# A hybrid attention and RG-LRU layer: each engine's order from a list scheduler in the kernel, in place of orders set by hand

## The chip, the cores and the metric

The kernel runs on one core of one Trainium2 chip. A core has five engines that run their own instruction streams in order and wait for each other through semaphores: PE (TensorE, matmuls; PEld is its weight loading), DVE (VectorE), ACT (ScalarE), POOL (GpSimd) and SP (SyncE, which only issues DMAs here). The metric is the device time in microseconds (us).

## The reference

One decoder layer on 2048 tokens of width 1024, in float32 (BATCH = DEPTH = 1). A mixer of eight attention heads and an RG-LRU recurrence share one input and one output projection; an MLP follows; both have RMS norms before and after.

```python
def hybrid_mixer(h, ...):
    z = h @ w_in                                   # 1024 x 2560
    q, k, v, xr, gr = jnp.split(z, [512, 1024, 1536, 2048], axis=-1)
    attn = dilated_attention(q, k, v)              # 8 heads of 64, patterns (128,1), (512,4), (2048,16)
    xr = causal_depthwise_conv(xr, conv_w, conv_b) # width 4
    rec = rg_lru(xr, w_r, b_r, w_i, b_i, lam) * jax.nn.gelu(gr)
    return jnp.concatenate([attn, rec], axis=-1) @ w_out

def rg_lru(x, ...):   # gates from block-diagonal products of x
    r = sigmoid(x @ w_r + b_r); i = sigmoid(x @ w_i + b_i)
    log_a = -8.0 * r * softplus(-lam)
    a = exp(log_a); u = sqrt(-expm1(2 * log_a)) * (i * x)
    # h[t] = a[t] * h[t-1] + u[t], an associative scan over the sequence

def reference(x, ...):
    h = rms_norm(x, mix_norm_pre)
    x = x + rms_norm(hybrid_mixer(h, ...), mix_norm_post)
    h = rms_norm(x, mlp_norm_pre)
    a = jax.nn.relu(h @ w1)                        # 1024 x 4096
    return x + rms_norm((a * a) @ w2, mlp_norm_post)
```

## The kernel before

**Products.** A float32 product is made of three matmuls: each operand is split into a high and a low part (fp32r), and high*high, high*low and low*high are added up in PSUM. The split is a cast on ACT for the high part (`split`, L54) and a subtraction on DVE or POOL for the low part (L55). wH, wL are a weight's parts, hH, hL those of the scaled input, thA, tlA, thB, tlB those of the attention probabilities.

**Tokens.** They are handled in two halves (hf 0 and 1) of 1024, each in two blocks b of 512. z_ct_b is a product of the input projection: column tiles 0 to 3 of 128 give q, 4 to 7 k, 8 to 11 v, 12 to 15 xr, 16 to 19 gr. Each has 8 x 3 matmuls of 512 columns (L198 to L200). The norm in front of it is applied afterwards: x is loaded in rows (xn, L145) for the sums of squares, `spread_norm` turns them into a broadcast tile bc with four small matmuls (pbc, L187), and bc multiplies the finished product. The operands themselves come from x transposed (xr_k, L167, eight loads of 256 KB for each block) and the gain g_sb.

**Recurrence** (`recurrent`). For each channel group c and block b: product 12+c, xr (DVE, L304), a first tap of the convolution on POOL (L307), three multiply-adds on DVE (xc, L310), the gate matmuls pr and pi on xc (L313, L315; their operands are plain float32), tanh, exp and sqrt on ACT, a scan on DVE (L331), and the gated output ge (L335 to L343, partly on POOL).

**Attention.** Per head, part A (S, local windows) and part B (SB, dilated): scores on PE (L557, L614, L615), row maximum with mask on DVE (L414), exponential on ACT (L420), transposes on PE (pT, L393), split on ACT and DVE, products with the values on PE (oA L581, oB L640), fold on ACT and DVE (L409). Halves of scores are numbered S_head_n and SB_head_c.

**The rest.** Output projection (m, L857 to L859), norm, then the MLP, whose first product (za, zb, zc, L1072 to L1074) and second product (o, L1222 to L1224) are each made by seven products of half-size blocks. The second half's attention runs while the first half's o products are under way.

**What sets the order.** The code writes steps in the order of three strings, with the letters q (a group of q, k and v products), r (a recurrence group), x (load and norm of a block) and a (a pair of heads):

```python
ORDER = "q00 r02 q01 a0 r03 q02 a1 q03 x2 x3 a2 q10 a3"
BETWEEN = "r10 r11 r12 r13"
LATER = "q11 q12 q13"
```

A scheduler of the framework that simulates a timeline (`schedule_with_timeline_sim=True`) orders the instructions of each engine from there. Two constructs override it. `tc.manual_schedule(engines=...)` keeps the code's own order: for PE from the output projection of the first half on, and for ACT, DVE and SP too while `interleave` mixes the second half's attention units with the first half's o products by counts written by hand. `tc.issue_after(ins)` keeps the instructions issued in it behind `ins` on the same engine. After that each engine works through its list in order.

## Time and profile before

| | |
|---|---|
| Runs | 2236.11 us median of 3 (2228.41, 2236.11, 2237.35) |
| Profiled execution | 2235.21 us; span from first to last instruction 2233.4 us |
| Mean granted TensorE clock | 0.988 |
| HBM traffic | read 337.09 MB, written 151.13 MB |
| Matmuls waited most for | gate products pr (L313), first operands of z (L198), values oB (L640) |

The time is that of the whole execution, the span ends with the last instruction; the two differ by 1.8 us. "Busy" counts the time in which an engine has an instruction under way; PE's matmuls overlap in the pipeline, so a matmul of 512 columns is listed with about 400 ns while the next starts some 225 ns after it.

### The profile page before, as it was taken

What the parts mean: (1) busy time and instruction counts of PE and PEld (TensorE: products, weight loads), DVE (VectorE), ACT (ScalarE), POOL (GpSimd) and SP (SyncE); (2) the same over time, 40 slices, a digit from 0 to 9 for tenths busy, and PEclk for the clock granted to TensorE, in tenths of its full rate; (3) what the DMA queues carried; (4) which work ended last, traced back from release to release, by engine and by line L of the source; (5) the groups of instructions that cost most, each with busy time, mean ns of one, the idle gap of its engine ahead of it and who ended that gap; (6) DMA issues with size and microseconds to landing.
All of it is one profiled execution on the core that took longest, in us unless ns stands there. A gap on an engine that the chain in (4) does not pass through costs nothing.

```text
span 2233.4 us, 30770 instructions
## 1 busy us (share of the span) xinstructions
PE 2155.4 (97%) x10264; PEld 1775.5 (79%) x10264; DVE 1507.1 (67%) x2910; ACT 1230.3 (55%) x2489; POOL 453.3 (20%) x536
## 2 busy tenths in 40 slices
PE   8999989989999999999999999999999999999998
PEld 6678878768788788888788787778878888888887
DVE  6767565987748867775667677778766566646456
ACT  7646464655434555554666666754455555654442
POOL 5543414555323000000001111113200000000003
PEclk9999999999999999999999999999999999999999
DMA  8365684555974676878777777777553434776665
GB/s 289 100 189 177 182 243 145 171 169 161 330 254 160 216 292 251 303 269 307 216 222 223 209 235 225 230 232 229 184 187 127 175 134 165 288 227 195 192 196 179
DMA packets 224116, 473.51 MB, mean 212 GB/s; under 512 B 23428, under 2 KB 78756, under 8 KB 217684
## 3 DMA queue, kind: packets, MB, share of 16 engines
q1 hardware_dynamic: 195140, 337.52, 47.9%
q0 software_dynamic: 28816, 134.01, 17.0%
q8 instruction: 81, 1.33, 0.2%
q14 instruction: 79, 0.65, 0.1%
HBM read 337.09 MB, written 151.13 MB: 219 GB/s over the span
## 4 chain that ended last, share of the span: by engine, by line
PE 68%; DVE 12%; DMA 7%; ACT 4%; issue 3%; POOL 1%; SPq 1%; DVEq 0%; ACTq 0%; POOLq 0%
PE o L1223 8%; PE o L1222 8%; PE o L1224 8%; PE za L1073 4%; PE za L1074 4%; PE za L1072 4%; PE z L198 3%; PE z L199 3%; PE z L200 3%; PE m L859 2%; PE m L858 2%; PE m L857 2%; PE zc L1073 2%; PE zc L1072 2%; PE zc L1074 2%
## 5 line engine op out<-in xcount | busy, mean ns | idle before, releaser
L198 PE MATMUL z<-hH,wH 128*128 128x512 f32 x640 | 262.4, 410 | 16.2 <-ACT wH L54 8.6
L199 PE MATMUL z<-hL,wH 128*128 128x512 f32 x640 | 259.7, 406 | 0.0
L200 PE MATMUL z<-hH,wL 128*128 128x512 f32 x640 | 258.7, 405 | 0.5 <-DVE wL L55 0.5
L198 PEld LDWEIGHTS z<-hH,wH 128*128 128x128 f32 x640 | 123.3, 193 | 51.7 <-ACT wH L54 9.2
L199 PEld LDWEIGHTS z<-hL,wH 128*128 128x128 f32 x640 | 123.2, 193 | 29.4 <-issue 4.1
L200 PEld LDWEIGHTS z<-hH,wL 128*128 128x128 f32 x640 | 122.9, 192 | 29.4 <-issue 4.6
L420 ACT ACTIVATE smB<-smB,stB 128x128 f32<-128x128 f32 (+3 forms) x128 | 71.6, 560 | 88.8 <-DVE stB L414 88.7
L1077 ACT ACTIVATE sq<-sq 128x512 f32<-128x512 f32 x93 | 58.8, 633 | 97.5 <-DVE sq L1081 97.5
L55 POOL TENSOR_TENSOR wL<-wraw,wH 128x512 fp32r<-128x512 f32 x58 | 83.3, 1452 | 78.0 <-ACT wH L54 75.2
L55 DVE TENSOR_TENSOR tlB<-pT_B,thB 128x384 fp32r<-128x384 f32 x96 | 57.0, 598 | 51.6 <-ACT thB L54 48.7
L1137 POOL DMA_DIRECT2D sa<-sq x31 | 16.5, 533 | 360.7 <-ACT sq L1078 350.1
L54 ACT CAST wH<-wraw 128x512 fp32r<-128x512 f32 (+1 forms) x81 | 47.2, 611 | 62.7 <-DMA wraw<-in_dram 31.9
L420 ACT ACTIVATE sm<-sm,stA 128x256 f32<-128x256 f32 (+1 forms) x128 | 63.1, 495 | 29.3 <-DVE stA L414 28.9
L1078 ACT ACTIVATE sq<-sq 128x512 f32<-128x512 f32 x124 | 76.1, 628 | 1.8
L1256 POOL TENSOR_TENSOR y<-y,g4b 128x512 f32<-128x512 f32 x8 | 12.4, 1583 | 259.3 <-ACT junk_y L84 259.3
L414 DVE CUSTOM_DVE_ANT_0 smB<-SB,mask_b 128x128 f32<-128x128 f32 (+3 forms) x128 | 59.2, 482 | 7.0 <-PE pT_B L393 6.3
L55 DVE TENSOR_TENSOR tlA<-pT,thA 128x512 fp32r<-128x512 f32 (+1 forms) x64 | 42.3, 669 | 26.1 <-ACT thA L54 25.8
L54 ACT CAST thB<-pT_B 128x384 fp32r<-128x384 f32 x96 | 48.4, 509 | 18.2 <-PE pT_B L393 10.8
L393 PE MATMUL pT_B<-ident,smB 128*128 128x128 f32 x320 | 52.3, 280 | 2.8 <-DVE nb L409 1.7
L414 DVE CUSTOM_DVE_ANT_0 sm<-S,mask_a 128x256 f32<-128x256 f32 (+1 forms) x128 | 47.4, 409 | 9.4 <-PE pT L393 4.0
L1072 PE MATMUL zc<-hHT,f_7H 128*128 128x512 f32 x128 | 50.1, 391 | 2.8 <-ACT hHT L54 2.8
L640 PE MATMUL oB<-thB,vb 128*128 128x256 f32 x192 | 46.5, 273 | 6.2 <-ACT thB L54 5.3
(608 smaller groups left out, 7035.0 us busy)
## 6 DMA issues: line engine op xcount, KB each, us to landing
sa<-as POOLq DMA_DIRECT2D x31, 1024.0 KB, 6.3
w1r<-in_dram SPq DMA_DIRECT2D x56, 512.0 KB, 4.2
sa<-sq POOLq DMA_DIRECT2D x31, 768.0 KB, 4.0
wraw<-in_dram SPq DMA_DIRECT2D x79, 256.0 KB, 3.8
place<-in_dram SPq DMA_DIRECT2D x14, 1024.0 KB, 7.6
sb<-place POOLq DMA_DIRECT2D x14, 1024.0 KB, 5.4
kh<-sk SPq DMA_DIRECT2D x24, 512.0 KB, 5.2
kl<-sk SPq DMA_DIRECT2D x24, 512.0 KB, 6.5
```

Source lines behind the costliest of these rows:

```text
L55: (lo_eng or nc.vector).tensor_tensor(out=lo, in0=src, in1=f32(hi), op=ALU.subtract))
L198: pe.matmul(z, hi[:, k, :], hh, start=(k == 0), stop=False)
L199: pe.matmul(z, hi[:, k, :], hl, start=False, stop=False)
L200: pe.matmul(z, lo[:, k, :], hh, start=False, stop=(k == KT - 1))
L414: v.tensor_tensor_reduce(out=sm[:, c0:c0 + w], in0=sp[:, c0:c0 + w], in1=mask[:, mask.shape[-1] - w:], scale=1.0, scalar=3.0e38, op0=ALU.a ...
L420: s.activation(out=sm[:, c0:c0 + w], in_=sm[:, c0:c0 + w], func=AF.Exp, scale=-1.0, bias=st[:, 0, u, cols[j]:cols[j] + 1], accum_out=st[:, ...
L1072: pe.matmul(o, hi[:, k], bh[:, k], start=start and k == 0, stop=False, skip_group_check=True)
L1073: pe.matmul(o, hi[:, k], bl[:, k], start=False, stop=False, skip_group_check=True)
L1074: pe.matmul(o, lo[:, k], bh[:, k], start=False, stop=k == KH - 1, skip_group_check=True)
L1222: pe.matmul(o, ah[:, ts], bh, start=fresh and j == 0, stop=False, skip_group_check=True)
L1223: pe.matmul(o, ah[:, ts], bl, start=False, stop=False, skip_group_check=True)
L1224: pe.matmul(o, al[:, ts], bh, start=False, stop=j == NJ - 1, skip_group_check=True)
```

## The change

The framework's context is wrapped in a class `Plan`. `manual_schedule` does nothing any more, and `issue_after` only records its pairs. When the whole program has been written, `Plan.run` works out from tiles and addresses which instruction depends on which, and hands them to `Machine`, which simulates the engines with cost formulas of its own (`cost`, `transfer`). At each moment an engine takes, of the instructions that are ready by that simulation, the one with the smallest `need`: the number, in the order of the code, of the first PE instruction that depends on it, directly or through others, or that waits for a buffer that it frees (at most 600 above its own number). A PE instruction's `need` is its own number. Loads whose `need` lies more than 400 PE instructions ahead wait. The resulting order of every engine is then fixed by dependencies from each instruction to the next. What is computed, and with which instructions, stays the same; the added helper lines move line numbers by 2, and those of `trunk` and below by 474.

```diff
+WINDOW = 400
+LAG = 600
+SLACK = 0.8
+BACKLOG = 4.0
...
+class Plan:
...
+    def manual_schedule(self, engines):
+        return contextlib.nullcontext()
+
+    @contextlib.contextmanager
+    def issue_after(self, ins):
+        traced = self.nc.cur_bb.bb.instructions
+        n = len(traced)
+        yield
+        self.behind += [(i.name, ins.name) for i in self.nc.cur_bb.bb.instructions[n:] if i.engine == ins.engine]
...
+    def run(self):
+        ins = [i for i in self.nc.cur_bb.bb.instructions if i.engine in ENGINES and i.outs]
...
+        order = Machine(ins, eng, acc, first, issued, self.taken, self.slots, held, guards).run()
+        info = mybir.DependencyInfo(mybir.DependencyClass.NoSync, mybir.DependencyReason.DATA)
+        for seq in order.values():
+            for a, b in zip(seq, seq[1:]):
+                self.tc.add_manual_dep(ins[b], ins[a].name, info, reason="plan")
...
+class Machine:
...
+        self.need = [n] * n
+        for _ in range(3):
+            for k in reversed(range(n)):
+                after = self.then[k] + [j for g in self.gates[k] for j in self.then[g]] + follow[k]
+                self.need[k] = k if eng[k] == "PE" else min([self.need[j] for j in after], default=n)
+        self.need = [min(x, k + LAG) for k, x in enumerate(self.need)]
...
+    def offer(self, k):
...
+        load = isinstance(self.ins[k], mybir.InstDMACopy) and self.acc[k][-1][6]
+        if load and self.need[k] > self.edge():
+            heapq.heappush(self.far, (self.need[k], k))
+            return
+        heapq.heappush(self.ready[e], (self.need[k], k))
+        self.poke(e)
...
+    def issue(self, e):
...
+        while self.ready[e]:
+            _, k = heapq.heappop(self.ready[e])
...
+        self.order[e].append(k)
...
+    def finish(self, k, pe):
+        slack = SLACK if k < self.n else 0
...
+        for j in self.then[k]:
+            if pe is None and slack and j < self.n and self.eng[j] == "PE":
+                self.at(self.now + slack, self.free_one, j, k)
...
+    def cost(self, k):
...
+            if f:
+                hold = 0.11 if n == P and i.is_transpose else 0.00174 * n
+            else:
+                hold = {P: 0.083, 2 * P: 0.121, 3 * P: 0.174}.get(n, 0.000446 * n)
...
+    def transfer(self, k):
...
+        rate = 6.0 if src[0] and dst[0] else 2.8 if dst[0] else 3.2 if run >= 512 else 4.8
...
     with tile.TileContext(nc, schedule_with_timeline_sim=True) as tc:
-        trunk(tc, *args, out)
+        plan = Plan(tc)
+        trunk(plan, *args, out)
+        plan.run()
```

The orders below are the rows of one engine's instruction list, with line, operation, output and inputs. Numbers behind a name tell tiles apart.

Three places show how instructions move. The first is SP's list at the very start of the program, before. xr_k are the blocks of transposed x, wraw_12 the raw weights of z_12.

```order
L167 DMA xr_0_287<-in_dram 128x512
L169 DMA g_sb<-in_dram 128x8
L126 DMA wraw_12_0_285<-in_dram 128x256
L167 DMA xr_1_297<-in_dram 128x512
L167 DMA xr_2_306<-in_dram 128x512
L167 DMA xr_3_312<-in_dram 128x512
```

The same place now, SP's first eleven rows; xn_j are the rows of x for the sums of squares, of the first block (366 to 375) and of the second (464 to 473).

```order
L147 DMA xn_0_366<-in_dram 128x1024
L147 DMA xn_1_369<-in_dram 128x1024
L147 DMA xn_2_372<-in_dram 128x1024
L147 DMA xn_3_375<-in_dram 128x1024
L169 DMA xr_0_287<-in_dram 128x512
L147 DMA xn_0_464<-in_dram 128x1024
L147 DMA xn_1_467<-in_dram 128x1024
L147 DMA xn_2_470<-in_dram 128x1024
L147 DMA xn_3_473<-in_dram 128x1024
L171 DMA g_sb<-in_dram 128x8
L128 DMA wraw_12_0_285<-in_dram 128x256
```

The eight xn loads have moved ahead of the gain and of the first weights; before, the first of them stood in row 17. PE's list, too, now begins with the four pbc of the first block.

The second place is DVE's list in the first recurrence groups, before, at the convolution of channel group 1, block 1 (xc_1_1). The xr_1_1 that it reads is made in row 89, the rows here are 114 to 121; a, th, i and ge are steps of other groups.

```order
L342 SCALAR_TENSOR_TENSOR ge_0_1_759<-ge_0_1_759,gr_0_1_757 128x512
L330 TENSOR_TENSOR i_0_1_719<-i_0_1_719,th_0_1_721 128x512
L228 TENSOR_TENSOR zn_4_1_1063<-z_4_1_1038,bc_501 128x512
L331 SCALAR_TENSOR_TENSOR xc_0_1_708<-r_0_1_717,state,i_0_1_719 128x512
L310 SCALAR_TENSOR_TENSOR xc_1_1_796<-xr_1_1_792,cw,xc_1_1_796 128x512
L332 COPY state<-xc_0_1_708 128x1
L343 SCALAR_TENSOR_TENSOR ge_0_1_759<-ge_0_1_759,xc_0_1_708 128x512
L310 SCALAR_TENSOR_TENSOR xc_1_1_796<-xr_1_1_792,cw,xc_1_1_796 128x512 x2
```

The same convolution now, rows 102 to 111 of DVE.

```order
L306 TENSOR_TENSOR xr_1_1_792<-z_13_1_767,bc_501 128x4x128
L334 COPY state<-xc_1_0_620 128x1
L345 SCALAR_TENSOR_TENSOR ge_1_0_671<-ge_1_0_671,xc_1_0_620 128x512
L328 TENSOR_TENSOR a_0_1_724<-r_0_1_717 128x512
L331 SCALAR_TENSOR_TENSOR i_0_1_719<-i_0_1_719,xc_0_1_708 128x512
L312 SCALAR_TENSOR_TENSOR xc_1_1_796<-xr_1_1_792,cw,xc_1_1_796 128x512
L329 SCALAR_TENSOR_TENSOR th_0_1_721<-a_0_1_724,th_0_1_721 128x512
L312 SCALAR_TENSOR_TENSOR xc_1_1_796<-xr_1_1_792,cw,xc_1_1_796 128x512
L344 SCALAR_TENSOR_TENSOR ge_0_1_759<-ge_0_1_759,gr_0_1_757 128x512
L312 SCALAR_TENSOR_TENSOR xc_1_1_796<-xr_1_1_792,cw,xc_1_1_796 128x512
```

The three multiply-adds have moved up to within nine rows of their xr_1_1, each with one other step between.

The third place is PE's list in the middle of head 5 of the first half, before; z_16_1 is a product of a recurrence group of the second half.

```order
L615 MATMUL SB_5_2_0_3728<-kl_5_3574,qs_5_3572 128x128
L614 MATMUL SB_5_2_0_3728<-kh_5_3573,qs_5_3572 128x256
L615 MATMUL SB_5_2_0_3728<-kl_5_3574,qs_5_3572 128x256
L199 MATMUL z_16_1_4690<-hL_2_3307,wH_16_4539 128x512
L200 MATMUL z_16_1_4690<-hH_2_3306,wL_16_4540 128x512
L393 MATMUL pT_0_5_1_0_3642<-ident,sm_5_4_3631 128x128 x4
L393 MATMUL pT_0_5_1_1_3659<-ident,sm_5_6_3650 128x128 x4
L198 MATMUL z_16_1_4690<-hH_3_3312,wH_16_4539 128x512
```

The same scores now:

```order
L395 MATMUL pT_0_5_1_0_3642<-ident,sm_5_4_3631 128x128 x2
L617 MATMUL SB_5_2_0_3728<-kl_5_3574,qs_5_3572 128x128
L616 MATMUL SB_5_2_0_3728<-kh_5_3573,qs_5_3572 128x256
L583 MATMUL oA_5_0_3618<-thA_3593,va_2_3359 128x256
L583 MATMUL oA_5_0_3618<-tlA_3594,va_2_3359 128x256
L617 MATMUL SB_5_2_0_3728<-kl_5_3574,qs_5_3572 128x256
```

The products of the recurrence are gone from between the scores, transposes and values of the head: those of heads 4 and 5 stand in rows 1321 to 1517 of PE's list together with 24 matmuls of z_0_0, where before they began in row 1265 and ended in row 1761.

382 lines of the change are left out of this document (added).

## The prediction

> **What bounds the kernel now.** I read the page's busy times and the clock row first, to see how much there is to win at all.
>
> ```profile
> PE 2155.4 (97%) x10264; PEld 1775.5 (79%) x10264; DVE 1507.1 (67%) x2910; ACT 1230.3 (55%) x2489; POOL 453.3 (20%) x536
> core 0: 2233.4 us, clock 0.988
> ```
>
> TensorE (PE) is busy for 2155.4 of 2233.4 us. The change removes no matmul, so two things can shrink: the 78.0 us in which PE idles, and the time its clock was held back, (1 - 0.988) x 2233.4 = 26.8 us of full-speed work. Together they bound any gain at 4.7%.
>
> Next come the windows of 50 us, which show where those two lie. Columns: window, its length, then busy us (instructions) of PE, PEld, DVE, ACT and POOL, then granted clock, DMA share, GB/s.
>
> ```profile
> 100.00:150.00 50.00, 46.03 (x183) 34.84 (x184) 31.46 (x48) 25.58 (x40) 19.77 (x21) 0.93 0.66 200
> 300.00:350.00 50.00, 43.67 (x246) 36.84 (x245) 28.88 (x83) 28.83 (x74) 10.23 (x9) 0.93 0.78 229
> 450.00:500.00 50.00, 43.14 (x185) 32.34 (x185) 41.35 (x60) 27.85 (x49) 30.59 (x29) 0.90 0.48 159
> 500.00:550.00 50.00, 48.55 (x237) 38.83 (x236) 44.63 (x79) 28.80 (x53) 22.93 (x25) 0.97 0.48 150
> 1050.00:1100.00 50.00, 45.86 (x228) 38.51 (x227) 23.92 (x56) 26.30 (x59) 0.00 (x0) 0.93 0.81 236
> 1350.00:1400.00 50.00, 45.63 (x249) 37.38 (x248) 39.26 (x96) 36.34 (x77) 6.10 (x11) 0.97 0.74 214
> 1400.00:1450.00 50.00, 45.28 (x240) 37.76 (x239) 35.35 (x83) 35.37 (x77) 6.01 (x9) 0.97 0.78 232
> 1450.00:1500.00 50.00, 45.42 (x230) 37.23 (x230) 33.78 (x65) 26.31 (x52) 5.13 (x10) 0.97 0.71 211
> 1650.00:1700.00 50.00, 50.00 (x222) 41.39 (x221) 34.24 (x54) 30.15 (x55) 4.27 (x8) 1.00 0.46 171
> ```
>
> The last row is the undisturbed case, from the MLP: 222 matmuls of 512 columns in 50 us, 0.225 us each, at full clock. The eight rows above lose PE time and clock, and all lie in the recurrence or in attention; no other engine is full there (the highest is DVE with 44.63 of 50). So what is lost is lost by order: PE's next instruction is waiting while the engine that should feed it does something else first. The table of PE's waits (us in total, times, longest) names the operands.
>
> ```profile
> PE z L198 <- ACT wH L54: 8.6, 3, 5.4
> PE pr L313 <- DVE xc L310: 6.1, 2, 3.5
> PE pr L313 <- DVE state L332: 3.9, 1, 3.9
> PE pr L313 <- ACT i L320: 3.5, 1, 3.5
> PE oB L640 <- ACT thB L54: 5.3, 4, 2.1
> PE z L198 <- DVE zn L228: 4.7, 2, 3.2
> PE pT L393 <- ACT sm L420: 4.1, 1, 4.1
> ```
>
> The gate products pr of the recurrence alone wait 6.1 + 3.9 + 3.5 = 13.5 us in four places.
>
> **The change, part by part.** Instructions, matmuls and bytes stay; only the orders move. I cost six places.
>
> *1. The start: a loss.* The scheduler ranks everything by the number that its first dependent PE instruction has in program order, and the code emits the pbc matmuls (which need the squares of xn) before any product. So SyncE now issues eight xn loads and one xr load before g_sb and the first weights; before, the first weights were its third transfer, and the xn loads began at row 17.
>
> ```profile
> 5.45 0.80 PE L198 MATMUL z<-hH,wH 128*128 128x512 f32 x1 [5.45 <-ACT wH L54]
> 12.27 3.60 SPq L145 DMA_DIRECT2D xn<-in_dram  x4
> xn<-in_dram SPq DMA_DIRECT2D x16, 512.0 KB, 6.1
> 15.00:20.00 5.00, 5.00 (x22) 3.51 (x21) 4.79 (x13) 4.11 (x8) 0.00 (x0) 1.00 1.04 404
> 20.00:25.00 5.00, 5.00 (x24) 4.15 (x23) 3.39 (x21) 4.56 (x9) 0.19 (x1) 1.00 1.04 392
> 25.00:30.00 5.00, 5.00 (x24) 4.14 (x23) 2.11 (x3) 4.97 (x9) 4.05 (x6) 1.00 1.03 382
> PE pbc L187 <- DVE dg L186: 0.8, 1, 0.8
> ```
>
> PE's first matmul starts at 5.45 us (first row). In the windows from 15 to 30 us the DMA share is 1.03 to 1.04, so the transfers are the limit, at 382 to 404 GB/s. Eight xn of 512 KB are 4.19 MB, and at the mean of 393 GB/s that is 10.7 us put ahead of z_12_0's operands. Some comes back: the same bytes no longer compete later, when PE waits for pbc (0.8 us) and about as much again for late operands. I take **+8.5**. The bounds: +4, if part of it is repaid by a faster stretch from 15 to 34 us, since the same bytes have to land by then in both orders; +13, if the early rate is that of a mixed stretch (229 GB/s, the 300 to 350 row, would make it 18, but there not only large loads run).
>
> *2. The recurrence: a gain.* Here the second excerpt of the orders matters. Before, the multiply-adds that finish xc_1_1 stand 29 rows behind the xr_1_1 that they read, behind state and output steps (ge, scan) of other channels that PE needs much later. The rows show DVE around the stall, two windows of 2 us there, and the least, median and greatest duration of such a multiply-add:
>
> ```profile
> 92.68 1.69 DVE L331 TENSOR_TENSOR_SCAN xc<-r,state,i 128x512 f32<-128x512 f32 x1
> 94.29 1.71 DVE L310 SCALAR_TENSOR_TENSOR xc<-xr,cw,xc 128x512 f32<-128x512 f32 x1
> 95.99 1.83 DVE L343 SCALAR_TENSOR_TENSOR ge<-ge,xc 128x512 f32<-128x512 f32 x1
> 98.00:100.00 2.00, 0.00 (x0) 0.00 (x0) 1.97 (x2) 0.00 (x0) 2.00 (x3) 1.00 0.05 17
> 102.00:104.00 2.00, 2.00 (x4) 0.94 (x3) 0.49 (x1) 1.73 (x3) 0.11 (x1) 0.50 0.69 268
> L310 DVE SCALAR_TENSOR_TENSOR xc<-xr,cw,xc x48: 732/752/3575, 40.8 to 519.7; 128x512 f32<-128x512 f32 x48
> ```
>
> Now the three multiply-adds come 5 to 9 rows behind their xr. Each pr stands 21 to 57 matmuls behind the end of its own product (4.8 to 13 us at 0.225 us for 512 columns). Three multiply-adds at 1.71 us, as in that row, are 5.1 us; at the median of 0.752, 2.3. So most of the 13.5 us goes. It does not all go: in the second half's recurrence DVE carries 41 to 45 of 50 us (rows 450 and 500), and an instruction that is placed just when its operand is due has little to spare. I leave 5: **-8.5** (from -13.5 to +5). The clock comes along: 50 x (0.07 + 0.10 + 0.03) = 10 us of full-speed work were lost in the rows from 100, 450 and 500; with waits of half the size I leave 4: **-6** (from -10 to 0).
>
> The stall shows how: PE at rest from 98 to 100 us, then clock 0.50 from 102 to 104 us. [...] But the row from 300 to 350 us does not: the longest wait in it is the 2.0 us of this row,
>
> ```profile
> PE z L198 <- ACT wH L54: 2.0, 1, 2.0
> ```
>
> and its clock is 0.93 all the same. [...]
>
> *3. Attention of the first half, heads 4 and 5: a small loss.* Before, their scores stand in blocks of four to eight among products of later groups, over some 500 rows of PE's order. Now both heads run in one cluster: 222 matmuls from S_4_0 to the last oB_5, some 24.5 us (their columns at 0.225 us per 512, and 0.083 us at least), of which only 24 are products of another group. The work of other engines per head comes from the groups of instructions, which cover 16 heads:
>
> ```profile
> L420 ACT ACTIVATE smB<-smB,stB 128x128 f32<-128x128 f32 (+3 forms) x128 | 71.6, 560 | 88.8 <-DVE stB L414 88.7
> L420 ACT ACTIVATE sm<-sm,stA 128x256 f32<-128x256 f32 (+1 forms) x128 | 63.1, 495 | 29.3 <-DVE stA L414 28.9
> L54 ACT CAST thB<-pT_B 128x384 fp32r<-128x384 f32 x96 | 48.4, 509 | 18.2 <-PE pT_B L393 10.8 <-PE oB L640 6.6
> L54 ACT CAST thA<-pT 128x512 fp32r<-128x512 f32 (+1 forms) x64 | 35.5, 568 | 6.0 <-PE pT L393 2.5 <-PE oA L581 1.8 <-DVE stB L414 0.9
> L420 ACT ACTIVATION_READ_ACCUMULATOR sm<-sm,stA 128x1 f32 x128 | 24.0, 188 | 0.0
> L420 ACT ACTIVATION_READ_ACCUMULATOR smB<-smB,stB 128x1 f32 x128 | 24.0, 188 | 0.0
> ```
>
> They add up to 266.6 us, 16.7 per head on ACT as a mean over both halves; the first half's tiles are the smaller ones, so for it 16.7 is an upper bound. Two heads are 33.4 us of ACT against 24.5 us of PE: PE idles 8.9, and I add 3.5 of clock: 12.4. The row from 300 to 350 us already pays 6.3 + 3.5 = 9.8 there. Net **+2.5** (from -6, if ACT's smaller tiles make the cluster balanced, to +12, if heads 0 to 3 also run bare in part).
>
> *4. The second half's attention: a gain at its start.* PE waited 4.1 us for sm once; the row from 1050 shows 4.1 idle and 3.5 of clock. SyncE's new order puts vb_0, qs_1 and place (2 MB) ahead of kl_0, which makes kl_0 later, by 6.5 us if those 2.1 MB go at about 320 GB/s (an estimate between the 236 of that row and the 404 above). But PE now has some 60 o matmuls, 13.5 us, between the first two scores and the rest. I take 7.6 down to 2: **-5.5** (from -7.6 to +6.5).
>
> *5. The rest of it, 1350 to 1500 us.* Idle 4.4 + 4.7 + 4.6 = 13.7 us and clock 3 x 1.5 = 4.5, many waits of 1 to 2 us (thB: 5.3 us in four). Values of part B now stand one to seven o matmuls later, 0.2 to 1.6 us. I take a quarter: **-5** (from -14 to +5). The fullest of the other engines, DVE, has 79% there, so there is no bound in throughput.
>
> *6. Weights and transposed keys.* Of the 8.6 us that z waited for wH, 5.4 is the start; 3.2, and 4.7 for zn, are left. **-3** (from -6 to +4). The MLP stays at its 222 matmuls per window: **0**, since there is no idle time that an order could take or add, and DVE has 34 and ACT 30 of 50 us there.
>
> Sum: +8.5 - 8.5 - 6 + 2.5 - 5.5 - 5 - 3 = -17.0 us, from the profiled execution's 2235.2 us to 2218.2. That execution lies 0.9 us under the median of 2236.1, so I forecast **2219 us**, 0.8% faster. Changes under 0.5%, 11.2 us, count as no change.
>
> **The rivals.**
> *Slower: the first half's attention becomes bound by ACT.* In clusters without other products each head has up to 16.7 us of ACT against 12.2 of PE (half of 24.5), 4.4 us short. If all eight heads run bare, that is 35.6 us, plus 7 of clock, less the 9.8 paid now: +33 in place of +2.5, so 2219 + 30 = 2249. It ends slower by 0.5% once some 40 of these 43 us come true, so with seven heads or more. Against it: heads 0 to 3, 6 and 7 still have some products among them. For it: four of the new order's heads have few.
> *No difference: the stalls only move.* The orders follow estimated durations. The multiply-add of L310 takes 0.73 to 3.58 us, with POOL busy beside the slow ones, and where the estimate is short, pr waits again. Then steps 2's 14.5 us are not won: 2219 + 14.5 = 2233.
> *A larger gain.* Of 78.0 us idle, 5.4 are the lead-in and 6.7 the end,
>
> ```profile
> 2225.00:2233.40 8.40, 1.68 (x8) 1.04 (x6) 2.68 (x7) 0.98 (x3) 0.00 (x0) 0.83 0.33 123
> ```
>
> so 66 are waits. If the order leaves 25 of them and 10 of the 26.8 of clock, the gain is 41 + 17 - 8.5 = 49: 2187. For it: no engine is full anywhere.
> [...]
>
> **How the numbers follow.** My forecast 0.42 (its own range 2205 to 2229); the rule on the clock 0.06; the larger gain 0.10; stalls moved 0.22; ACT-bound clusters 0.20. Faster by more than 0.5% means below 2225: 0.36 of the forecast, 0.06 and 0.10, 0.52. Within 0.5% (up to 2247): 0.06 of the forecast, nearly all of "moved" and a little of the slower case, 0.28. Slower: 0.20. Range 2184 to 2256: from just under the larger gain to the slower rival with 7 us more, where start and clusters both cost their upper values.
>
> **What would show it.** Step 1: the first product some 8 to 13 us later than 5.45, behind pbc, with xn first in the queue. Step 2: pr's waits at 5 us in all, and clock 1.00 from 100 to 150 us. Step 3: idle PE with ACT near full somewhere between S_4_0 and oB_5. Step 4: no wait of 4 us for the first sm of the second half. The prediction is wrong if PE's idle time does not fall to about 65 us, or if waits grow in heads 0 to 3, where I see products enough.

## The result and the profile after: slower by 1.6%

The changed kernel takes 2270.23 us (median of 4; 2266.49 to 2275.13), the kernel before 2236.28 in the same comparison (4 runs). The ratio is 1.0161, with a 95% interval of 1.0129 to 1.0193: slower, where 0.8% faster was forecast, and outside the range of 2184 to 2256. The profiled execution took 2275.1 us, so it is 5 us above the median. Below, single executions are compared by stage and medians by total.

The page after, its busy times, and its line of cores:

```profile
PE 2165.4 (95%) x10264; PEld 1779.6 (78%) x10264; DVE 1508.4 (66%) x2910; ACT 1230.1 (54%) x2485; POOL 458.4 (20%) x536
core 0: 2273.4 us, clock 0.984
```

The other engines do the same work as before, to within 5 us. PE's idle time went from 78.0 to 2273.4 - 2165.4 = 108.0 us, and the clock lost (1 - 0.984) x 2273.4 = 36.4 us in place of 26.8. Idle time and clock give 30 + 10 = 40 us, the difference of the two spans. So all of the loss is PE waiting and PE running at a lower clock.

PE's waits after (rows left out are marked):

```profile
PE pbc L189 <- DVE dg L188: 20.0, 2, 19.5
PE pT_B L395 <- DVE tlB L57: 13.1, 6, 4.8
PE o L1225 <- DVE b_9L L1311: 9.6, 1, 9.6
PE S L559 <- DVE stA L416: 8.7, 3, 5.0
PE z L200 <- DVE state L334: 5.0, 2, 3.7
PE za L1074 <- ACT sq L1118: 4.9, 3, 2.4
PE z L200 <- DVE xr L306: 3.6, 3, 1.3
...
PE z L200 <- ACT wH L56: 2.8, 1, 2.8
...
PE pr L315 <- DVE xc L312: 1.9, 2, 1.1
...
PE pr L315 <- DVE state L334: 1.5, 2, 1.1
...
PE pr L315 <- POOL wL L57: 0.8, 1, 0.8
...
PE pT L395 <- ACT sm L422: 0.6, 1, 0.6
```

The waits of pr fell from 13.5 to 4.2 us, as forecast; 5.0 + 3.6 us stand beside them for products z in the same chains, where before there was one short row:

```profile
PE z L198 <- DVE xr L304: 0.7, 2, 0.4
```

So the chains of the recurrence wait 12.8 us in all, against 14.2. New are 19.5 us at the start, 13.1 for tlB, 9.6 for one o factor and 8.7 for the row maximum stA.

**Where the 40 us lie.** I count PE's work as each matmul times the median spacing of its shape in the trace of before, and call the start time of the matmul at a given amount of work, less that work, the lag. Both programs do the stages in the same sequence as far as a lag at such marks is concerned, but not matmul by matmul, so a stage's value is good to some us.

```
lag of PE (us) at PE work of   40   120   200   400   560  1000  1520  2040
before                       14.2  31.2  34.6  56.8  83.8  97.3 137.7 137.3
changed kernel               29.7  33.9  39.7  79.6 108.9 122.8 172.0 177.2
difference                   15.5   2.7   5.1  22.8  25.1  25.5  34.3  39.9
```

Four things stand out. The start loses 15.5 us and gets 12.8 back within 80 us of work. Between 200 and 400 us of work, the attention heads of the first half from head 2 on, 17.7 us are lost. From 400 to 560, most of the second half's recurrence and the products behind it, 2.3. From 1000 to 1520, the attention of the second half, 8.8 more (single executions of one order differ by as much there, see e10_mix), and 5.6 at the end, at the second half's MLP, where za waits for sq (2.4 us of it) and which I did not pursue.

**How a wait comes about.** The place of the 9.6 us, on DVE and on PE (timelines; start, length, in brackets the idle time before and what ended it):

```profile
1520.32 0.69 DVE L1311 TENSOR_TENSOR b_8L<-b_8L,b_8H 128x512 fp32r<-128x512 f32 x1
1526.18 0.69 DVE L720 TENSOR_TENSOR na<-na,co 128x512 f32<-128x512 f32 x1 [5.17 <-DMA co<-sco]
...
1528.64 0.69 DVE L723 TENSOR_TENSOR nb<-nb,co 128x512 f32<-128x512 f32 x1 [1.17 <-DMA co<-sco]
...
1533.62 0.68 DVE L1311 TENSOR_TENSOR b_9L<-b_9L,b_9H 128x512 fp32r<-128x512 f32 x1
```

```profile
1534.36 0.79 PE L1225 MATMUL o<-b_9L,a_9H 128*128 128x512 f32 x1 [9.56 <-DVE b_9L L1311]
```

b_9H, from which b_9L is made, was ready at 1523.1 us. But DVE stood at na, which waits for a transfer (co), and b_9L stood nine instructions further back in its queue. By the list scheduler's clock, co should have landed before na came up. The same at 325 us, with xr: ACT, DVE and PE in turn.

```profile
325.46 0.72 ACT L174 ACTIVATE hH<-xr,g_sb 128x512 fp32r<-128x512 f32 x1 [5.94 <-DMA xr<-in_dram]
```

```profile
326.22 2.38 DVE L175 SCALAR_TENSOR_TENSOR hL<-xr,g_sb,hH 128x512 fp32r<-128x512 f32 x1 [5.32 <-ACT hH L174]
328.52 0.68 DVE L230 TENSOR_TENSOR zn<-z,bc 128x512 f32<-128x512 f32 x1
329.12 0.28 DVE L416 CUSTOM_DVE_ANT_0 sm<-S,mask_a 128x128 f32<-128x128 f32 x1
```

```profile
329.90 0.55 PE L559 MATMUL S<-kh,qa 128*128 128x256 f32 x1 [4.98 <-DVE stA L416]
```

PE had the scores ready for DVE's maximum, which needs no xr at all; it stood behind one that does. In neither place does DVE take anything ahead of the instruction that waits: it idles 5.2 us before na, with b_9H there for the last 3.1 of them, and 5.3 us before hL, with the first four scores there for the last 3.6 (PE had written them by 322.6 us). For 256 KB of xr the scheduler's formula gives 1.2 us, 0.8 (3.2 us per MB) and 0.55 for the signal, about 2.6 us if nothing else moves; the view of this source line between 295 and 375 us gives a median of 5.3 (min/median/max).

```profile
DMA to landing us min/median/max: 3.5/5.3/7.0
```

### The profile page after: what moved, and what is told of

Its sections match the earlier page's. It is cut to its first block, busy times and chain, and to the rows that moved or that the text cites. A ratio compares the mean times of both kernels' runs of the same rounds, so it can differ in the third digit from the quotient of the medians.

```text
span 2273.4 us, 30859 instructions
## 1 busy us (share of the span) xinstructions
PE 2165.4 (95%) x10264; PEld 1779.6 (78%) x10264; DVE 1508.4 (66%) x2910; ACT 1230.1 (54%) x2485; POOL 458.4 (20%) x536
## 4 chain that ended last, share of the span: by engine, by line
PE 64%; issue 10%; DMA 9%; DVE 8%; ACT 5%; POOL 3%; SPq 1%; DVEq 0%; POOLq 0%; ACTq 0%
PE o L1225 6%; PE o L1226 6%; PE o L1224 6%; PE za L1074 5%; PE za L1075 5%; PE za L1076 5%; PE z L200 3%; PE z L201 3%; PE z L202 3%; PE zc L1074 2%; PE zc L1075 2%; PE zc L1076 2%; PE m L861 2%; PE m L859 2%; PE m L860 2%
## 5 line engine op out<-in xcount | busy, mean ns | idle before, releaser
L57 POOL TENSOR_TENSOR wL<-wraw,wH 128x512 fp32r<-128x512 f32 x58 | 85.3, 1486 | 36.3 <-ACT wH L56 29.3
L422 ACT ACTIVATE sm<-sm,stA 128x256 f32<-128x256 f32 (+1 forms) x128 | 63.3, 496 | 31.7 <-DVE stA L416 31.4
L395 PE MATMUL pT_B<-ident,smB 128*128 128x128 f32 x320 | 58.8, 287 | 14.0 <-DVE tlB L57 13.1
L1258 POOL TENSOR_TENSOR y<-y,g4b 128x512 f32<-128x512 f32 x8 | 12.4, 1579 | 252.2 <-ACT junk_y L86 252.2
L1234 DVE TENSOR_TENSOR y<-o,y 128x512 f32<-128x512 f32 x24 | 16.0, 684 | 69.0 <-PE o L1226 69.0
L395 PEld LDWEIGHTS pT_B<-ident,smB 128*128 128x128 f32 x320 | 38.4, 144 | 24.9 <-DVE tlB L57 13.0
L312 DVE SCALAR_TENSOR_TENSOR xc<-xr,cw,xc 128x512 f32<-128x512 f32 x48 | 53.9, 1122 | 5.0 <-POOL xc L309 4.8
L56 ACT CAST thB<-pT_B 128x384 fp32r<-128x384 f32 x96 | 48.9, 511 | 14.5 <-PE pT_B L395 7.9
```

The source lines that it names most:

```text
L57: (lo_eng or nc.vector).tensor_tensor(out=lo, in0=src, in1=f32(hi), op=ALU.subtract))
L395: pe.transpose(t[:, i * P:(i + 1) * P], blk, ident)
L422: s.activation(out=sm[:, c0:c0 + w], in_=sm[:, c0:c0 + w], func=AF.Exp, scale=-1.0, bias=st[:, 0, u, cols[j]:cols[j] + 1], accum_out=st[:, ...
```

## Experiments

All times are medians, all ratios against the kernel before in the same comparison, with 95% intervals. The changed kernel's 2270.2 comes from the first comparison, the others ran later; the kernel before read 2234.7 to 2236.5 in all of them.

### First: the start, transfers, hand order, the cluster

**e1_start** ranks the two pbc behind products:

```diff
-                self.need[k] = k if eng[k] == "PE" else min(...)
+                self.need[k] = late.get(k, k) if eng[k] == "PE" else min(...)
+        # late: pbc0 -> first matmul of z0_17_0, pbc1 -> first of z0_12_1
```

> The scheduler's order, except that the pbc matmuls of the first two blocks are ranked behind products (need of the first matmul of z_17_0 and of z_12_1), so that SP issues xr and the first weights ahead of xn, as before. If the start is an independent loss: first product near 5 us in place of 25.3, and the lag of 15 us that the changed kernel has at 40 us of PE work is gone; 2270 down to about 2257. If the start's lag only absorbs waits that come later anyway (at 120 us of work only 2.7 us of it were left): under 5 us gained, 2265 or more.

Measured: 2268.77 us, ratio 1.0151 (1.0132 to 1.0170). The first product starts at 5.4 us, and the lag at 40 us of work is 22.4 in place of 29.7 (14.2 before), so that about half of the start's loss is mended. At 120 us it is 31.7, against 33.9. That half was real and almost all of it is absorbed: 1.5 us in the medians.

**e2_late4** makes every transfer 4 us longer in the scheduler:

```diff
-        return (1.2 if self.eng[k] == "SP" ...
+        return 4.0 + (1.2 if self.eng[k] == "SP" ...
```

> The scheduler assumes every transfer to take 4 us longer than in its formula; nothing else. Theory L (instructions that wait for a transfer are placed too early, and hold up everything behind them in their engine's queue): DVE's and ACT's long waits for DMA (5.2 us for co twice, 5.3 and 5.9 for xr, 7.0 for a_12L) shrink, and PE's waits for tlB (13.1 us), b_9L (9.6) and stA (8.7) fall by half or more: 2270 down to 2245 to 2255. Rival H (the loss comes from giving up the hand-written interleaving): no change within 6 us, since no hand order comes back.

Measured: 2340.32 us, ratio 1.0465 (1.0446 to 1.0484). PE's waits for tlB and b_9L did shrink, to under 3.4 us each, but one new wait is worth more than all of them:

```profile
PE S L559 <- DVE stA L416: 38.0, 7, 33.1
```

There DVE takes factor steps (L1150), each behind a transfer of place (it idles 9.4 and 9.5 us before two groups of them), ahead of the row maximum. So it is the same kind of stall at another place. Between 200 and 400 us of work the lag grew by 28 us in place of 40, as Theory L has it, but neither expected time came. The theory's blunt remedy failed; here an estimate that is wrong in the other direction cost 70 us.

**e3_hand** keeps the code's order where the kernel before kept it by hand:

```diff
     def manual_schedule(self, engines):
-        return contextlib.nullcontext()
+        return self.region(engines)   # records its instructions, engine by engine
 ...
     def offer(self, k):
+        if k in self.before and not self.started[self.before[k]]:
+            self.chain[self.before[k]] = k
+            return
```

> The scheduler as in the change, but it must keep the code's order where the kernel before kept it by hand: on PE from the first half's output projection on, and on ACT, DVE and SP in the interleaving of the second half's attention. Rival H: the 9 to 18 us that the changed kernel loses between 1040 and 1240 us of PE work and the later 6 and 5 us go: about 2258, with the stretch from 1040 to 1520 us of work as before. Theory L: a hand order has no mistaken placement of transfers' consumers there either, so this run alone also gains there, but the stretch from 200 to 400 us of work, where the lag grows by 18 us, stays as it is; only the run with longer transfers changes both.

Measured: 2259.43 us, ratio 1.0106 (1.0089 to 1.0123), 10.8 us back. Between 1000 and 1520 us of work the lag grows by 35.1 us, against 40.4 before and 49.2 after the change. Rival H accounts for a part: the hand order is worth some 11 us. The stretch from 200 to 400 stays as it was (36.8), as expected by L.

**e5_a2** puts one group of products ahead of heads 4 and 5 in the code:

```diff
-ORDER = "q00 r02 q01 a0 r03 q02 a1 q03 x2 x3 a2 q10 a3"
+ORDER = "q00 r02 q01 a0 r03 q02 a1 q03 x2 x3 q10 a2 a3"
```

> The order string has q10 ahead of a2 in place of behind it, so that heads 4 and 5 of the first half rank behind the products z_0, z_4 and z_8 of the second half. If the cluster without products (step 3 of the prediction) is what costs the 18 us between 200 and 400 us of PE work: 2270 down to 2255 to 2260. If it is the late xr loads of the second half that hold up ACT and DVE, the cluster only moves and waits for xr remain or grow, since the products that need them now come first: 2268 to 2280.

Measured: 2267.39 us, ratio 1.0142 (1.0122 to 1.0161). Between 200 and 400 us of work the lag grows by 38.7 in place of 39.9: moving the cluster by one group of products does not help, and new waits for pbc and stA (3 us each) appear near 340 us. The time lies just outside the second expectation and far from the first.

### Second: named transfers, POOL's price, sums

```diff
+        late = 6.0 if any(b[5] and str(b[6]).startswith(("xr2_", "xr3_", "co0_", "co1_")) for b in boxes) else 0.0
-        return (1.2 if self.eng[k] == "SP" ...
+        return late + (1.2 if self.eng[k] == "SP" ...
```

is e6_named;

```diff
-            return last, last            # POOL in cost()
+            return 1.15 * last, 1.15 * last
```

is e7_pool; e8_hand_start has e1 and e3 together, e9_mend all four edits (e1, e3, e6, e7).

**e6_named**

> The change, but the scheduler assumes 6 us more for two kinds of loads only: xr of the second half's blocks (tiles xr2, xr3) and the weights co of the attention's join. Theory L in its narrow form (consumers of these loads stand too early in ACT's and DVE's queues): the waits that the trace ties to them go, 5.0 us for stA near 325 us, 9.6 us for b_9L near 1524 us, 2.8 us for tlB near 1233 us, and nothing comes in their place: 2270 down to 2250 to 2256. If a list order trades one such stall for another, as with 4 us on every transfer: those three go, but the time stays at 2262 or above.

Measured: 2260.19 us, ratio 1.0118 (1.0103 to 1.0133), 10.0 us back. The three waits went. tlB still waits elsewhere, and the rest of PE's largest after the start are others:

```profile
PE pT_B L395 <- DVE tlB L57: 10.2, 8, 4.3
PE vt L242 <- DVE zn L230: 7.1, 2, 6.1
PE S L559 <- DMA kh<-sk: 5.3, 1, 5.3
...
PE z L200 <- DVE gr L337: 4.2, 1, 4.2
```

The 9.6 us on b_9L became 3.1 us on b_10H, and the stretch from 1360 to 1520 us of work shrank from 14.3 to 7.4 us of lag. Near xr it was a trade: no wait for stA at 325 us, 5.3 for kh at 360. Both expectations hold in part. By the stages the gain lies in the second half, where only co is priced anew: the lag grows by 33.0 us from 1000 to 1520 in place of 49.2. The two prices were not run apart.

**e7_pool**

> The change, but every POOL operation is priced 15% longer in the scheduler: the trace has 1.49 us for a wL subtraction, its formula 1.29. Theory L extended to engines: the wait of 3.1 us for stA near 259 us, where DVE stands at ge, whose chain waits for POOL, goes, and the pr and state waits (8 us in all) shrink: 2270 down to 2262 to 2266. If the mispricing does not matter: 2270 within 3 us.

Measured: 2273.97 us, ratio 1.0180 (1.0156 to 1.0204): no gain. The wait of 3.1 us near 259 us did go, and the lag at 400 us of work is 66.0 in place of 79.6; at 560 it is 108.1, as if nothing had happened. What is gained at the heads is lost again behind them. That pointed to the next group.

**e8_hand_start**

> The order kept by hand, as in the run before, and the start mended, both together, otherwise the scheduler of the change. If the start's gain is absorbed by the recurrence (1.5 us was left of it) and the hand order's is not (10.8): 2257 to 2259. If they are independent of what follows: 2250.

Measured: 2258.51 us, ratio 1.0106 (1.0090 to 1.0123): the first expectation, 0.9 us for the start beside the hand order.

**e9_mend**

> Hand order, start, 6 us on xr2, xr3 and co, and 15% on POOL, all together. Theory L with its parts additive: 2259 - 1.5 - 5 (the xr stall) - 4 (POOL) - 2 (what co still costs under the hand order) = 2246, still above 2236, since the shift from 400 to 640 us of PE work and the 5.5 us near 1930 us are touched by none of them. If one stall only takes the place of another: 2256 to 2260.

Measured: 2252.48 us, ratio 1.0078 (1.0060 to 1.0097), between the two. The lag at 400 us of work is 61.0, near that of before (56.8), and then grows by 41.3 us to 560, where before it grew by 27.0. I put this down to the recurrence of the second half, which the lag does not bear out: some 17 of the 41.3 us (5 before) lie between 520 and 560 us of work, behind the recurrence, where one wait of PE for vt takes 7.4 us.

### Third: the recurrence among the heads

DVE and POOL after the change, in the windows of the last heads (6 and 7) and of the recurrence behind them (PE, PEld, DVE, ACT, POOL busy us, then clock):

```profile
400.00:450.00 50.00, 48.62 (x307) 40.02 (x305) 39.70 (x111) 36.50 (x99) 14.42 (x13) 1.00 0.20 58
450.00:500.00 50.00, 42.86 (x161) 31.23 (x160) 48.63 (x53) 21.76 (x28) 40.95 (x40) 0.93 0.53 168
```

Before, the window from 450 to 500 us had 41.35 us of DVE and 30.59 of POOL. The heads took ACT and little POOL here (36.50 and 14.42 of 50 us), the recurrence DVE and POOL (48.63 and 40.95). With the heads done first, DVE was full at 48.6 of 50 us; from that I drew Theory R below. But PE is no worse off in this window than before: it is busy for 42.86 us at a clock of 0.93, where the prediction's row has 43.14 at 0.90.

**e10_mix** changes the code's order and nothing in the scheduler:

```diff
-ORDER = "q00 r02 q01 a0 r03 q02 a1 q03 x2 x3 a2 q10 a3"
-BETWEEN = "r10 r11 r12 r13"
+ORDER = "q00 r02 q01 a0 r03 q02 a1 q03 x2 x3 q10 r10 a2 r11 r12 a3 r13"
+BETWEEN = ""
```

> The change, but the code is written in another order, which the scheduler's ranks follow: the recurrences r10 to r13 of the second half stand among the last attention heads of the first (q10 r10 a2 r11 r12 a3 r13) in place of behind them. Theory R (after the change the second half's recurrence has no attention beside it, and stands on DVE, 48.6 of 50 us busy between 450 and 500 us): the lag grows by 20 us or less between 400 and 560 us of PE work in place of 29, and the time is 2258 to 2264. Rival: that stretch is bounded by the transfers of 550 to 650 us (DMA share 0.85 and 0.92), which have to be through in any order: the lag at 560 us of work stays at 105 or more, 2268 to 2274.

Measured: 2249.35 us (five executions, 2247.7 to 2264.0), ratio 1.0082 (1.0050 to 1.0115), 20.9 us back, more than Theory R had given. The same window:

```profile
450.00:500.00 50.00, 45.93 (x262) 37.18 (x261) 42.75 (x117) 37.15 (x96) 33.01 (x34) 1.00 0.51 165
```

PE is busy for 45.93 us in it in place of 42.86, at full clock, and DVE for 43 in place of 49. The lag grows by 26.8 us from 200 to 400 us of work (39.9 after the change) and by 24.9 from 400 to 560 (29.3): 17.5 us together. The rival is refuted, the lag at 560 being 91.2. But Theory R's own mark, 20 us or less from 400 to 560, is missed too, and 13.1 of the 17.5 us lie ahead of it, where the heads are. The rows of heads 4 and 5, from the first score of head 4 to the last values of head 5, before, after the change and in this run, show why:

```profile
304.50:415.50 111.00, 104.67 (x585) 88.42 (x584) 71.50 (x181) 65.78 (x160) 41.48 (x41) 0.97 0.69 209
321.50:368.90 47.40, 36.84 (x232) 33.07 (x231) 36.61 (x110) 35.73 (x103) 8.34 (x9) 0.86 0.65 201
328.90:431.00 102.10, 95.54 (x497) 77.53 (x496) 65.82 (x149) 56.33 (x132) 41.33 (x40) 1.00 0.60 192
```

In PE's lists 278 matmuls of products z stand in this stretch before, 24 after the change and 281 in this run. PE's idle time and the lost clock come to 9.7, 17.2 and 6.6 us. So the recurrences placed among the heads give the heads their products back. e5_a2, which differs from this run in the place of the recurrences alone, has 148 products there and ended 18 us slower. I did not try whether the new order string would make the kernel before faster, too.

The second half's lists of PE, DVE, ACT and SP, compared over the last 4327, 1397, 1016 and 463 rows, are identical to those of the changed kernel; the lag there still grows by 40.1 in this execution and by 49.2 in that one. So one execution of one order differs by some 9 us from another there, and stage values of the second half from single traces are read no finer than that. In the first half it is less: e3_hand has the changed kernel's lists up to the output projection, and its lag at 400 and 560 us of work is within 4 us of that kernel's.

**e11_mend_mix** adds all the mending to it.

> All the mending of the run before (hand order, start, 6 us on xr2, xr3 and co, 15% on POOL) and the recurrences among the last heads. Theory R: 2252 less some 10, 2240 to 2245, as there the lag grows by 41 us between 400 and 560 us of PE work. Rival, transfers bound: 2250 to 2256.

Measured: 2242.32 us, ratio 1.0026 (1.0012 to 1.0040): the time of the first expectation. One wait of 11.2 us for the load va is new, at 322 us.

**e12_nohand** is the kernel before, without its hand orders:

```diff
-        with per, tc.manual_schedule(engines={mybir.EngineType.PE}):
+        with per:
-                    with tc.manual_schedule(engines={mybir.EngineType.Activation, mybir.EngineType.DVE, mybir.EngineType.SP}):
+                    with contextlib.nullcontext():
```

> The kernel before, with the two hand orders taken out (PE from the first half's output projection on; ACT, DVE and SP in the interleaving): there the framework's scheduler decides alone, as it did for the first half. If the second half's hand order is worth the same 11 us against any scheduler: 2247. If the list scheduler's ranks and prices are what loses them: 2236 within 4 us.

Measured: 2313.91 us, ratio 1.0349 (1.0329 to 1.0369), beyond both expectations: under the framework's scheduler the hand order is worth 78 us. One wait there alone is longer than any after the change:

```profile
PE m L857 <- ACT m_4H L54: 21.2, 1, 21.2
```

So among schedulers without hand orders the new one is the better by 44 us. It lost against the framework's scheduler with them.

**e13_slack3**

```diff
-SLACK = 0.8
+SLACK = 3.0
```

> The change with SLACK 3.0 in place of 0.8: the scheduler offers a matmul to PE 3 us after the operand is ready by its own clock. If PE's waits come from placing each matmul just when its operand is due: waits fall from 108 us in all to 90 or less and 2270 becomes 2255 or less. If they come from operations that stand behind a late one in ACT's and DVE's queues for 5 to 10 us: little changes, 2265 to 2275.

Measured: 2275.64 us, ratio 1.0176 (1.0153 to 1.0199). No gain: PE idles 109 us in place of 108, and the time is just past the upper end of the second expectation. So the moment at which a matmul is offered to PE is not the point. That the queues of ACT and DVE are is not shown by this run, only by the timelines above.

### Fourth: do the parts add up

Four more, all with the recurrence among the heads and the hand order: e14_mix_hand_start with the start, e15_mix_hand without it, e16_mix_hand_start_co with 6 us on co alone, and e17_mix2, which is e14 with

```diff
-q10 r10 a2 r11 r12 a3 r13
+q10 a2 r10 r11 a3 r12 r13
```

> Recurrences among the last heads, hand order and start, with the scheduler's own prices. If the parts add up: 2249 - 11 - 1 = 2237, level with the kernel before. If pricing xr, co and POOL matters beside them as it did without the mix (6 us between the runs e8 and e9): 2243 or more.

> As the run before it without the mended start. If the start is absorbed by waits that follow within 120 us of PE work: within 3 us of it. If the mix has removed the waits that absorbed it: 5 us or more slower.

> Mix, hand order and start, and 6 us more on the loads of co alone. If the price on xr made the wait of 11.2 us for va (the loads of va then stand behind others on SP): that wait is gone and the time is 2232 to 2238. If it comes from elsewhere: 2240 or more.

> As e14, but q10 a2 r10 r11 a3 r12 r13 in place of q10 r10 a2 r11 r12 a3 r13. If what counts is only that heads and recurrence overlap, within 4 us of e14. If each recurrence has to stand ahead of the heads that fill its waits: 5 us or more above e14.

Measured: e14 2241.66 us, ratio 1.0027 (1.0015 to 1.0039); e15 2247.97, 1.0052 (1.0033 to 1.0072); e16 2239.21, 1.0015 (1.0002 to 1.0028); e17 2249.90, 1.0056 (1.0041 to 1.0071).

The parts nearly add up: mix and hand order and start give 28.6 of the 34 us (e14 lies between its two expectations), and co 2.5 more, with intervals that overlap. In e16 the wait for va is gone, though its time is not in the range that went with that; in e14 there is none either, so the wait came with the price on xr or on POOL, I can't say which. The start is worth 6.3 us in the medians here (e15 against e14), where it was worth 1.5 and 0.9, as the second expectation has it. But the intervals overlap, so that this is not clear of noise, and in the profiled executions the lag of e15 is only 2.7 us above that of e14 at 560 us of work and 0.4 at 1520. And 8.2 us lie between e17 and e14: that heads and recurrence overlap is not enough, here the recurrence has to stand ahead of the heads. e16 is the fastest with the list scheduler; it is not faster than the kernel before, and no other version is.

## Why the prediction was wrong

The sum was -17 us, +34 came out.

- **Step 1, the start: +8.5.** The first product starts at 25.3 us, 19.8 later than before, where I had said 8 to 13, and the loss of 15.5 us at 40 us of work is larger than the bound of +13. At 120 us of work 2.7 of it is left; e1, which mends about half, gains 1.5 us. I costed the transfers alone. The rest is ACT's queue, which I had not read: ACT stood at sp, which needs a small load (vec_lam) behind the others, and then took the second block's squares before the first cast.

```profile
15.55 0.20 ACT L268 ACTIVATE sp<-sp 128x4 f32<-128x4 f32 x1 [5.22 <-DVE sp L267]
...
24.03 0.71 ACT L174 ACTIVATE hH<-xr,g_sb 128x512 fp32r<-128x512 f32 x1
```

What this hH reads had landed by 18.2 us (xr_0 at 11.7, the gain g_sb at 18.2). And what is late at the start was not carried to the end: I counted it in full, where the recurrence behind it, which lost time before too, absorbed nearly all.
- **Step 2, the recurrence: -14.5.** Right for pr by itself, 4.2 us of waits left where I said 5, and for the first of the three clock rows:

```profile
100.00:150.00 50.00, 49.13 (x211) 38.44 (x210) 31.54 (x39) 23.23 (x35) 26.45 (x31) 1.00 0.81 246
```

The row from 450 to 500 us went from 0.90 to 0.93 only. And the 8.5 us of waits were not won: the products z in the same chains wait 8.6 us now, and the chains 12.8 in place of 14.2.
- **Step 3, heads 4 and 5: +2.5, and this is the step that failed.** I saw that the heads had come apart from the products, and costed ACT's throughput alone. What I put at nothing is what PE waits for when ACT or DVE stand at an instruction whose operand is late, with no product at hand for PE meanwhile. Between 200 and 400 us of work the lag grew by 17.7 us more than before. Heads 4 and 5 are 7.5 of it: idle time and lost clock of 17.2 us (forecast 12.4) against 9.7 before. In this ACT did fill up, as the step has it, and PE idled:

```profile
350.00:355.00 5.00, 4.44 (x33) 3.67 (x32) 4.43 (x21) 4.95 (x17) 0.00 (x0) 1.00 0.56 182
355.00:360.00 5.00, 2.73 (x17) 2.08 (x18) 4.36 (x14) 4.95 (x15) 0.00 (x0) 0.93 0.41 144
```

But the longest wait in these heads, 5.0 us at 325 us, came before that from a load of xr, with ACT idle for 5.9. Another 4.9 us lie in the row from 250 to 300 us, before and after, in heads 2 and 3:

```profile
250.00:300.00 50.00, 50.00 (x300) 43.76 (x299) 28.65 (x94) 30.66 (x88) 17.69 (x16) 1.00 0.65 204
250.00:300.00 50.00, 46.56 (x303) 40.38 (x302) 32.19 (x102) 34.06 (x98) 17.77 (x17) 0.97 0.65 202
```

There I had seen "products enough"; PE waits 3.1 us for stA at 259 us, as DVE stands at ge. The other 5 us I did not trace. e10 puts products back among the heads and gains 20.9 us. My reading at that time, that the recurrence had become bound by DVE, is not borne out by the lag: from 400 to 560 us of work the changed kernel loses 2.3 us against before.
- **Steps 4 and 5: -10.5.** The 4.1 us for sm went, as I said (0.6 left). But I took for granted that a new order would shorten the many small waits by a quarter. That failed, too: they became fewer and longer, tlB 13.1 us, b_9L 9.6; the three longest of tlB and the one of b_9L each go back to a load at the head of ACT's or DVE's queue (a_12L, a_9L, co and co). e3 shows that giving up the hand order costs 10.8 us.
- **Step 6: -3.** About right: of the waits of z for wH only one of 2.8 us is left, and it is at the start, so that the 3.2 us elsewhere went. But its 0 for the MLP, "since there is no idle time that an order could take or add", failed: 5.6 us were added there.
- **The rivals.** "The stalls only move" comes nearest to what happened, but I priced it at no net change. Nothing in it said that new stalls can be longer than the old ones. On the clock, no run shows that only a long idle stretch in one piece costs it (the rule on the clock, with 0.06 of the chances). Two rows that lose clock do hold long single waits, of 5.0 us and of 9.6 us:

```profile
300.00:350.00 50.00, 44.05 (x244) 38.18 (x243) 31.01 (x85) 26.86 (x71) 16.75 (x14) 0.93 0.71 220
1500.00:1550.00 50.00, 40.40 (x184) 32.30 (x183) 34.83 (x61) 26.09 (x46) 6.23 (x12) 0.90 0.82 251
```

A third row loses as much clock as the second without such a wait:

```profile
350.00:400.00 50.00, 44.73 (x228) 36.85 (x228) 26.05 (x69) 23.34 (x61) 17.85 (x15) 0.90 0.61 184
```

Its longest wait is 1.9 us. PE was busy for 1.26 of the 3.4 us from 355.9 on, in short pieces, and the granted clock was 0.51 in the 3.4 us after that. So several short waits close together cost clock here as one long wait does. It was so in the prediction's row from 300 to 350 us, too: PE was busy for 1.41 of the 3.4 us from 326.0 on, where the longest wait is 2.0 us, and the clock was 0.50 in the 3.4 us after that. The last section has the count over all runs.

The parts, measured: 20.9 us for the recurrence's place, 10.8 for the hand order, 10.0 for the price of xr and co, 1.5 for the start, each alone on the changed kernel. They overlap, since together they are over 34. That these orders and prices cost so much is shown by the runs; what each did in the queues I read from single places in the traces. Open are the last 3 us to the kernel before, the 5.6 us at za in the second half's MLP, which stay in nearly all versions, which of the prices made va wait, and whether the new order string would help the kernel before.

## What to carry to other kernels

A scheduler that ranks by what TensorE needs first can take away the work that fills its waits: count, for each stretch, what TensorE has left to do while one late operand holds up a queue, not only how full each engine is. A list order is only as good as its estimate of transfers: here an instruction placed at the moment when its load should land held up what stood behind it in its queue (DVE idled 5.2 us before na, ACT 5.9 us before hH), and a general safety margin of 4 us per transfer cost 70 us more than it saved. Where a stretch was ordered by hand, keep that order as an input to the scheduler and drop it piece by piece, with a run for each.

## What the hardware showed that was not expected

The same order in the second half, row for row, took 9 us more in one execution than in another (lag growing by 49.2 and 40.1 us from 1000 to 1520 us of work), with the first halves ordered differently. And of a delay of 7.3 us at the start (the changed kernel against e1_start, at 40 us of work) 2.2 us were left 80 us of work later.

In these traces the granted clock went with how busy PE was, not only with single idle stretches. In the profiled executions of all 18 kernels here the granted clock falls to 0.50 for 3.4 us or a multiple of it, 213 times ahead of the end. In the 3.4 us just before each fall PE was busy, by the profile, for at most 66% of the time, in 212 cases for at most 59%. Windows of the same length on the same grid at full clock with no fall behind them had PE busy for at least 44%, leaving out the first 35 us. In the traces before and after alone there are 13 and 14 such falls, right after windows with PE busy for at most 58% and 49%, and the windows with no fall behind them had PE busy for at least 49% and 44%. So in these traces each such window with PE busy for less than 44% was followed by a fall, the one from 355.9 us after the change (37%, longest wait 1.9 us) among them.
